# Sample-state updates that multiply 32 rows of keys and values in place of 128 masked ones, and pools that change hands in fewer steps

## The chip, the cores and the metric

The kernel runs on one core of a Trainium2 chip. The metric is the time of one execution on the device in microseconds, the median of several runs. TensorE is called PE, VectorE DVE, ScalarE ACT, GpSimd POOL and SyncE SP; SP and POOL issue the transfers between HBM and SBUF. PSUM, into which PE writes its sums, has eight banks of 512 float32 values in each of 128 partitions.

## The reference, cut to what matters

Two layers over 576 columns: 512 tokens of one prompt and 8 tokens of each of 8 sample rows. The first layer is a gated short convolution, the second a block with a matrix memory of 4 heads. The change touches the part in which the memory of each sample row is brought up to date (for a sample row, one chunk of 8 tokens):

```python
def step(carry, inp):                 # one chunk; for a sample row the only one
    C, n, m = carry
    ...
    logw = g[..., None] - b + ij
    m_new = jnp.maximum(g + m, jnp.max(logw, axis=-1))
    decay = jnp.exp(g + m - m_new)
    kw = kj * jnp.exp(logw - m_new[..., None])[..., None]
    C_new = decay[..., None, None] * C + jnp.einsum('bhjd,bhje->bhde', kw, vj)
    n_new = decay[..., None] * n + jnp.sum(kw, axis=2)
...
out = ((hn * onorm_w) + skip * xc) * jax.nn.silu(z)
return out @ w_out, new_buf, C, n, m
```

C has 8 rows x 4 heads x 512 x 512 values, 32 MB that are read, changed and written. `bhjd,bhje->bhde` sums over the 8 tokens of one sample row.

## The kernel before, in words

Values are float32. Products that have to be exact are split into a high and a low part (`hi`, `lo` of the activations, `wh`, `wl` of the weights) and made of three products. The large products of both layers (`p`, L311, 288 columns; `acc`, L229, 256 and 320 columns) run on PE one behind another; ACT makes `wh` (L209) and DVE `wl` (L210) from raw weight buffers that SP loads (L215). The kernel ends with a third stage, from about 1280 us on, in which the z gates (`acc`), the numerators and final states of the prompt (`num`, `cp`, L1214 and L1215) and the sample states lie side by side on every engine.

**Sample states.** `value_stack` and `key_stack` make for each head and each half u of the 8 sample rows a stack of 128 rows: 4 sample rows x 32, where the 32 are the 8 tokens in four forms (high and low parts of keys against high and low parts of values), so that one product over the 32 rows is the whole sum. `stack` (L1061 to L1063) scales the loaded keys (`ld`, fetched by SP at L1072), casts them to `sth` and subtracts, which gives `kst` or `vst`. `pn` (L1099) sums the keys. Then four copies `km` are made (L1107), each with all rows but those of one sample row set to zero by the constant `gmask`. There are 32 units (head, u, and one of 4 blocks dt of 128 keys) and 64 calls of `piece`, two to a unit, each for two sample rows j: the product `r` (L1160: weights are 128 columns of `km`, 512 columns of `vst` stream past them) and on DVE `c = c*dec + r` (L1161). A half state `c` is loaded at L172 and stored at L1130, both by SP.

**Tiles of the array.** PE can use a part of its rows or columns for a matmul. The trace writes the shape behind the names: 128*128 is the whole array; `qa` (L799) uses 32 of the columns (128*32) and puts four groups side by side; the corrections `Rs` (L1035, L1039) use 16 rows (16*128).

**Buffers.** One pool `act` of slots with the tag T holds `kst`, `vst`, `km`, `sth` and most others. `accumulators` closes a PSUM pool and opens the next, and whoever uses a bank of the new pool first waits for the last use of what lay there before. `load_buffers` does the same for the raw weight buffers and what lies beside them (scratch `X` of the first layer, then the states `C`). It is done at the start, within the first layer (`acc0a`), before its output projection (`acc0b`, `loads1`), at the second layer (`acc1`) and before the last stage (`acc2`, `loads2`). `mark` (L377) writes once to four block banks. The order of the rest is set by hand-written queues (`stream`, `work`, `pops`) and a scheduler that orders the instructions of each engine.

Of the kernel before, what the change touches and what calls it, by code (L numbers as in the profile page):

```python
# [40 lines left out]
CST = {}  # L41
_n = 0
for _name, _cnt in (("ident", 128), ("ones", 128), ("causal", 128), ("smask", 256), ("sel", 64),
                    ("seln", 4), ("gmask", 4), ("k_low", 1), ("v_low", 1), ("v_one", 2)):
    CST[_name] = (_n, _cnt)
    _n += _cnt
NCST = _n
# [2 lines left out]
HT = NT // 2  # L50
# [2 lines left out]
H0 = 4  # L53
H1 = 2
WARM2 = 14
CBUF = 8
LAG = 6
AHEAD = 2
FH = 2
# [9 lines left out]
def trunk(tc, io):  # L69
    nc = tc.nc  # L70
    ctx = ExitStack()
    with ctx:
# [2 lines left out]
        const = ctx.enter_context(tc.tile_pool(name="const", bufs=1))  # L75
        small = ctx.enter_context(tc.tile_pool(name="small", bufs=2))
        accs = [None, None]

        def accumulators(name, **kw):

            if accs[0] is not None:
                accs[0].close()
            accs[0] = ctx.enter_context(ExitStack())
            accs[1] = accs[0].enter_context(tc.tile_pool(name=name, space=PSUM, **kw))

        loads = [None, None, 0]

        def load_buffers(name, raw):

            if loads[0] is not None:  # L90
                loads[0].close()
            loads[0] = ctx.enter_context(ExitStack())
            loads[1] = loads[0].enter_context(tc.tile_pool(name=name, bufs=1))
            loads[2] = raw

        def load_tile(name, tag):
            uid[0] += 1
            return loads[1].tile([P, 2, 512], F32, name=f"{name}{uid[0]}", tag=tag, bufs=loads[2] if tag == "raw" else CBUF - loads[2])

        dram = ctx.enter_context(tc.tile_pool(name="dram", bufs=1, space=DRAM))  # L100

        uid = [0]
        layer0 = [False]

        def X(n=NT, name="x"):

            if not layer0[0]:
                return T(n, name=name)
            uid[0] += 1
            return loads[1].tile([P, n], F32, name=f"{name}{uid[0]}", tag="X", bufs=7)  # L110

        def T(n=NT, dt=F32, name="t"):
            uid[0] += 1
# [3 lines left out]
        def R(n=NT, name="r"):  # L117
            return T(n, F32R, name)

        def mm(name="mm"):  # L120
            uid[0] += 1
            return accs[1].tile([P, 1024], F32, name=f"{name}{uid[0]}", tag="mm", bufs=2)

        def block(name="blk"):
            uid[0] += 1
            return accs[1].tile([P, 512], F32, name=f"{name}{uid[0]}", tag="blk", bufs=4)[:, 0:HT]

        def bank(name="b"):
            uid[0] += 1
            return accs[1].tile([P, 512], F32, name=f"{name}{uid[0]}", tag="b1", bufs=4)  # L130

        def S(shape, dt=F32, name="s", bufs=2):
            uid[0] += 1
# [16 lines left out]
        def c(name, a=0, b=None):  # L150
            o, n = CST[name]
            return cst[:, o + a:o + (n if b is None else b)]
# [329 lines left out]
                ins = nc.tensor.matmul(b[:, 0:256], warm[:, 0:128], warm, start=True, stop=True).ins  # L482
            return ins

        accumulators("acc0", bufs=2)
        load_buffers("loads0", 4)
        layer0[0] = True
        warm_up(WARM)
        nc.scalar.preload_act_table_set("silu_and_others")
# [3 lines left out]
        for k in range(KD):  # L493
# [3 lines left out]
            if k in (0, 3):  # L497
                for c_ in range(2):
                    i = 4 * (k // 3)
# [53 lines left out]
        for f in range(NW):  # L553
            if f % 4 == 0:
                ext = T(320, name="ext")
                load(out=ext, in_=io["exa"][f // 4])
            ext_f = ext[:, 80 * (f % 4):80 * (f % 4) + 80].rearrange("p (b t) -> p b t", t=10)
            u, cv = T(name="u"), T(name="cv")

            def gated(u=u, c_=cx[0], x=cx[1]):  # L560
                nc.vector.tensor_tensor(c_, c_, rb2, ALU.mult)
                nc.vector.tensor_tensor(u, x, c_, ALU.mult)

            def saved(u=u, cv=cv, f=f):
                nc.gpsimd.tensor_copy(cpa[:, f, :], u[:, NP - 2:NP])
                nc.vector.tensor_tensor(cv, cv, rb, ALU.mult)

            work.append(gated)
            work.extend(conv_steps(cv, u, ext_f, [col("ca0", f), col("ca1", f), col("ca2", f)]))
            work.append(saved)  # L570

            second = f in SECOND
            if second:
                block_weights(4 * f + 2, 4 * f + 3)
            zb = [raw_weights(4 * f + i) for i in (2, 3)] if f and not second else None
            if f + 1 < NW:
                cx = [T(name="cx") if f < 11 else X(name="cx") for _ in range(2)]
            if f == 0:
                for i in range(2):
                    acc = mm("acc")  # L580
                    products(acc, weights(4 + i), h1, True, True)
                    nc.scalar.copy(cx[i], flat(acc))
                    if i:
                        block_weights(8, 9)
                    first_blocks(2 + i)
                accumulators("acc0a", bufs=2)
                mark(h1[0][0][:, 0:P], h1[0][0][:, 0:HT])
            elif f + 1 < NW:
                block_pair(4 * f + 4, 4 * f + 5, fs, None, *cx, False, pops=1)
            run(len(work))  # L590
            if 0 < f < NW - 2:
                block_weights(4 * f + 8, 4 * f + 9)

            def product(i):
                if f == 0:
                    return raws[i]
                acc = mm("acc")
                products(acc, weights(4 * f + i, raw=zb[i - 2]), h1, True, True)
                return flat(acc)

            z = T(name="z")
            if second:
                b_ = T(name="b")
                block_pair(4 * f + 2, 4 * f + 3, fs, None, z, b_, False)
                za = z
            else:
                za = product(2)
            nc.vector.tensor_tensor(z, za, rb, ALU.mult)
            nc.scalar.activation(z, z, AF.Silu)
            nc.vector.tensor_tensor(cv, b_ if second else product(3), cv, ALU.mult)  # L610
            nc.vector.tensor_tensor(cv, cv, z, ALU.mult)
            ya.append(split(cv))
            if f % 4 == 3:
                store(out=io["exa_out"][f // 4], in_=ext)
        accumulators("acc0b", bufs=2)
        load_buffers("loads1", 4)
        layer0[0] = False
        store(out=io["cpa_out"], in_=cpa)

# [26 lines left out]
        for f in range(NW):  # L646
# [84 lines left out]
        kss = [dram.tile([P, 2, 512], F32, name=f"kss{h}") for h in range(NH)]  # L731

        xc, fc = [], []
        accumulators("acc1", bufs=4)
        mark(xm[0][0][:, 0:P], xm[0][0][:, 0:HT])

        def later_tile(f):
# [7 lines left out]
        for h in range(NH):  # L745
            vt = []
            for dt in (0, 2):
                f = 4 * h + dt
# [101 lines left out]
        for h in (3, 0, 1, 2):  # L850
            st = heads[h]
            for dt in range(4):
                f = 4 * h + dt
# [40 lines left out]
            if h in (3, 0, 1):  # L894
                work.extend(lambda h=h, i=i: query_state(heads[h], unit(h, *divmod(i, 4)), i) for i in range(8))

        accumulators("acc2", bufs=2)
        load_buffers("loads2", 2)
        zs = {h: [] for h in range(NH)}

        def z_tile(pops=()):
# [151 lines left out]
        seln = const.tile([P, 4], F32R, name="seln")  # L1053
# [37 lines left out]
        def key_stack(h, u):  # L1091

            st = heads[h]
            raw, = fetched.pop(("ks", h, u))
            o = R(512, "kst")
            stack(raw, G["s"][:, 1 + u, 32 + 4 * h:33 + 4 * h], c("k_low"), o)
            pn = bank("pn")
            for dt in range(4):
                nc.tensor.matmul(pn[:, 4 * dt:4 * dt + 4], o[:, 128 * dt:128 * dt + 128], seln, start=True, stop=True)  # L1099
            t = S([P, 4, 4], name="ns")  # L1100
            nc.gpsimd.tensor_tensor(t, nst[:, h, u], G["dec"][:, 8 * h + 4 * u:8 * h + 4 * u + 4].unsqueeze(1)
                                    .broadcast_to([P, 4, 4]), ALU.mult)
            nc.vector.tensor_tensor(nst[:, h, u], pn[:, 0:16].rearrange("p (d g) -> p d g", g=4), t, ALU.add)

            st[u] = [R(512, "km") for _ in range(4)]
            for g, t in enumerate(st[u]):
                nc.scalar.activation(t, o.bitcast(F32), AF.Copy, scale=c("gmask", g, g + 1))  # L1107


        ORDER = (2, 0, 1, 3)  # L1110
# [24 lines left out]
        def piece(n):  # L1135
# [21 lines left out]
            o = 8 * h + 4 * u + 2 * i  # L1157
            for j in range(2):
                r = bank("r")
                nc.tensor.matmul(r, kst[2 * i + j][:, 128 * dt:128 * dt + 128], vst[:, 0:512], start=True, stop=True)  # L1160
                ins = nc.vector.scalar_tensor_tensor(ct[:, j, :], ct[:, j, :], dec[:, o + j:o + j + 1], r,  # L1161
                                                     ALU.mult, ALU.add).ins
                if j == 0:
                    store_half(ins)
# [338 lines left out]
def _consts():  # L1503
# [3 lines left out]
    def put(name, a):  # L1507
        o, n = CST[name]
        cst[:, o:o + n] = a
# [14 lines left out]
    sel[:, 32:48] = p[:, None] % 32 == 4 + r[None, :]  # L1524
    put("sel", sel)
    put("seln", ((g[:, None] == np.arange(4)[None, :]) & (s[:, None] % 2 == 0)).astype(np.float32))
    put("gmask", (g[:, None] == np.arange(4)[None, :]).astype(np.float32))
    ka, va = (s < 2).astype(np.float32), (s % 2 == 0).astype(np.float32)
    put("k_low", (ka - 1)[:, None])
    put("v_low", (va - 1)[:, None])  # L1530
# [106 lines left out]
```

## Time and profile before

| | |
|---|---|
| median of 3 runs | 1700.97 us (1699.05 to 1701.9) |
| profiled execution, own time | 1701.48 us |
| its span in the trace | 1699.6 us |
| PE busy | 1666.6 us (98%) |
| DVE busy | 1074.5 us (63%) |
| ACT busy | 749.6 us (44%) |
| POOL busy | 98.6 us (6%) |
| mean granted clock of PE | 0.989 |

The span runs from the first to the last instruction of the trace; the time of the execution holds 1.9 us more around it. A busy row of PE counts overlapping matmuls once. Starts of neighbouring rows tell what a matmul adds, since the shown duration of one overlaps the next.

### The profile page before, as it was taken

What the parts mean: (1) busy time and instruction counts of PE and PEld (TensorE: products, weight loads), DVE (VectorE), ACT (ScalarE), POOL (GpSimd) and SP (SyncE); (2) the same over time, 40 slices, a digit from 0 to 9 for tenths busy, and PEclk for the clock granted to TensorE, in tenths of its full rate; (3) what the DMA queues carried; (4) which work ended last, traced back from release to release, by engine and by line L of the source; (5) the groups of instructions that cost most, each with busy time, mean ns of one, the idle gap of its engine ahead of it and who ended that gap; (6) DMA issues with size and microseconds to landing.
All of it is one profiled execution on the core that took longest, in us unless ns stands there. A gap on an engine that the chain in (4) does not pass through costs nothing.

```text
span 1699.6 us, 30928 instructions
## 1 busy us (share of the span) xinstructions
PE 1666.6 (98%) x12251; PEld 1583.9 (93%) x12251; DVE 1074.5 (63%) x1957; ACT 749.6 (44%) x1463; POOL 98.6 (6%) x241
## 2 busy tenths in 40 slices
PE   9999999999999999999999999999999999997998
PEld 8999999999999999999999899899898788897998
DVE  7988888874337975556644345344367567776775
ACT  5555555542234554444533233233245456554431
POOL 0000000000000000000010000000002100000000
PEclk9999999999999999999999999999999899998999
DMA  5222322314333444535433652642746587998993
GB/s 195 75 91 92 104 86 97 103 53 163 128 116 94 141 128 123 172 112 173 131 88 98 220 162 75 234 139 66 252 143 208 197 286 262 321 331 265 324 326 105
DMA packets 107488, 275.23 MB, mean 162 GB/s; under 512 B 11056, under 2 KB 33456, under 8 KB 107344
## 3 DMA queue, kind: packets, MB, share of 16 engines
q1 hardware_dynamic: 91984, 255.95, 45.8%
q10 hardware_dynamic: 15360, 17.32, 2.9%
q8 instruction: 96, 1.57, 0.4%
q14 instruction: 48, 0.39, 0.1%
HBM read 211.13 MB, written 62.09 MB: 161 GB/s over the span
## 4 chain that ended last, share of the span: by engine, by line
PE 91%; DMA 4%; DVE 2%; ACT 1%; issue 1%; SPq 0%; DVEq 0%; ACTq 0%
PE acc L229 31%; PE p L311 29%; PE p L387 17%; PE qa L799 2%; DMA c<-cs 2%; PE r L1160 1%; PE g L700 1%; PE cp L1214 1%; PE ta L719 1%; DMA cs_out<-c 1%; PE cp L1215 1%; PE blk L387 1%; PE s L818 1%; DMA wr<-wts 1%; PE s L819 0%
## 5 line engine op out<-in xcount | busy, mean ns | idle before, releaser
L311 PE MATMUL p<-hi,wh 128*128 128x288 f32 x1136 | 337.3, 297 | 0.0
L311 PE MATMUL p<-lo,wh 128*128 128x288 f32 x1136 | 334.0, 294 | 0.0
L311 PE MATMUL p<-hi,wl 128*128 128x288 f32 x1136 | 333.6, 295 | 0.0
L209 ACT CAST wh<-wr 128x512 fp32r<-128x512 f32 x262 | 161.8, 620 | 324.0 <-PE acc L229 170.7
L229 PE MATMUL acc<-hi,wh 128*128 128x256 f32 (+1 forms) x1328 | 290.2, 299 | 6.8 <-ACT num L1227 3.9
L210 DVE TENSOR_TENSOR wl<-wr,wh 128x512 fp32r<-128x512 f32 x262 | 179.5, 688 | 176.5 <-ACT wh L209 171.9
L229 PE MATMUL acc<-lo,wh 128*128 128x256 f32 (+1 forms) x1328 | 289.0, 298 | 0.0
L229 PE MATMUL acc<-hi,wl 128*128 128x256 f32 (+1 forms) x1328 | 288.3, 298 | 0.0
L229 PEld LDWEIGHTS acc<-hi,wh 128*128 128x128 f32 x1328 | 225.0, 191 | 12.4 <-ACT num L1227 4.1
L229 PEld LDWEIGHTS acc<-hi,wl 128*128 128x128 f32 x1328 | 224.3, 191 | 2.0 <-issue 1.7
L229 PEld LDWEIGHTS acc<-lo,wh 128*128 128x128 f32 x1328 | 224.8, 191 | 0.8 <-issue 0.6
L311 PEld LDWEIGHTS p<-hi,wh 128*128 128x128 f32 x1136 | 213.1, 188 | 6.3 <-ACT wh L209 5.0
L311 PEld LDWEIGHTS p<-hi,wl 128*128 128x128 f32 x1136 | 212.5, 188 | 3.8 <-issue 2.5
L311 PEld LDWEIGHTS p<-lo,wh 128*128 128x128 f32 x1136 | 213.3, 188 | 0.0
L257 ACT CAST wh<-wr 128x512 fp32r<-128x512 f32 x176 | 109.0, 619 | 200.5 <-PE p L311 99.6
L257 ACT CAST wh<-ws 128x512 fp32r<-128x512 f32 x132 | 81.9, 620 | 197.2 <-PE p L387 98.1
L258 DVE TENSOR_TENSOR wl<-wr,wh 128x512 fp32r<-128x512 f32 x176 | 121.3, 689 | 67.4 <-ACT wh L257 58.4
L387 PE MATMUL p<-hi,wl 128*128 128x288 f32 x736 | 160.1, 297 | 0.0
L387 PE MATMUL p<-hi,wh 128*128 128x288 f32 x736 | 159.7, 298 | 0.0
L387 PE MATMUL p<-lo,wh 128*128 128x288 f32 x736 | 159.7, 296 | 0.0
L258 DVE TENSOR_TENSOR wl<-ws,wh 128x512 fp32r<-128x512 f32 x132 | 91.0, 689 | 105.1 <-ACT wh L257 91.9
L387 PEld LDWEIGHTS p<-hi,wh 128*128 128x128 f32 x736 | 117.9, 188 | 9.7 <-issue 8.0
(382 smaller groups left out, 2582.2 us busy)
## 6 DMA issues: line engine op xcount, KB each, us to landing
wr<-wts SPq DMA_DIRECT2D x222, 512.0 KB, 3.7
c<-cs SPq DMA_DIRECT2D x112, 512.0 KB, 5.6
cs_out<-c SPq DMA_DIRECT2D x64, 512.0 KB, 6.7
x<-xT SPq DMA_DIRECT2D x16, 288.0 KB, 4.4
xcs<-xc ACTq DMA_DIRECT2D x16, 288.0 KB, 2.3
x<-xcs SPq DMA_DIRECT2D x16, 288.0 KB, 4.3
ld<-xcs SPq DMA_DIRECT2D x16, 288.0 KB, 8.0
cp_out<-cp ACTq DMA_DIRECT2D x16, 257.0 KB, 7.3
```

What stands on the lines that cost most here:

```text
L209: last_act[0] = nc.scalar.copy(hi, raw[:, 4 * i:4 * i + 4, :]).ins
L210: nc.vector.tensor_tensor(lo, raw[:, 4 * i:4 * i + 4, :], hi.bitcast(F32), ALU.subtract)
L229: nc.tensor.matmul(acc[:, o:o + j - i], a[:, k % 4, :], x[:, i:j], start=(first and k == 0 and p == 0), stop=(last and k == 7 and p == 2))
L257: last_act[0] = nc.scalar.copy(hi, src).ins
L258: nc.vector.tensor_tensor(lo, src, hi.bitcast(F32), ALU.subtract)
L311: nc.tensor.matmul(bank_, a[:, j, :], x, start=(start and j == 0 and i == 0), stop=(j == 3 and i == 2), skip_group_check=True)
L387: nc.tensor.matmul(b, a[:, k % 4, :], x[:, t:t + HT], start=bool(new) and k == 0 and i == 0, stop=(k == 7 and i == 2), skip_group_check=True)
L700: nc.tensor.matmul(g[32 * j:32 * j + 32, 0:b - a], w[:, 32 * j:32 * j + 32], tiles[j][:, a:b], start=True, stop=True)
L719: nc.tensor.transpose(pa[:, 128 * it:128 * it + 128], t[:, 128 * it:128 * it + 128], ident)
L799: nc.tensor.matmul(st["q"][32 * g:32 * g + 32, :], st["qp"][dt // 2][:, dt % 2, 128 * u + 32 * g:128 * u + 32 * g + 32], ct[g // 2][:, g % ...
L818: nc.tensor.matmul(sb[0], a[:, 0:128], b[:, 0:512], **ends)
L1160: nc.tensor.matmul(r, kst[2 * i + j][:, 128 * dt:128 * dt + 128], vst[:, 0:512], start=True, stop=True)
```

## The change

- The product `r` takes the 32 rows of its sample row, `kst[g]` and `vst[g]` with `g` 32 rows wide at 0, 32, 64 or 96, so the four sample rows use four row tiles of the array. The 32 copies `km`, their slots and `gmask` are gone.
- PSUM: block banks and the others have a pool each. The pool `acc0a` goes on through the output projection of the first layer, so `acc0b` is gone; there `bank()` takes block banks (`bank_tag`). `acc1` replaces the two wide accumulators alone, and the block banks that `mark` writes stay as they are.
- SBUF: the raw weight buffers `raw0` stay open over the first layer and its output projection; only the scratch X makes room for the states C (`scratch0`, `states1`). Before the last stage both are replaced (`raw2`, `states2`), as before.

```diff
+        bank_tag = ["b1"]
+        def accumulators(name, blocks=None):
+            for i in (1,) if blocks is None else (1, 0):
+                if accs[i] is not None:
+                    accs[i][0].close()
+                    accs[i] = None
+            for i in (0, 1) if blocks else (1,):
+                stack = ctx.enter_context(ExitStack())
+                accs[i] = stack, stack.enter_context(tc.tile_pool(name=f"{name}{i}", bufs=4, space=PSUM))
+        def load_buffers(tag, name, bufs=None):
+            for t in ("C", "raw") if tag == "raw" else ("C",):
+                if t in loads:
+                    loads.pop(t)[0].close()
+            stack = ctx.enter_context(ExitStack())
+            loads[tag] = stack, stack.enter_context(tc.tile_pool(name=name, bufs=1)), bufs
...
-            return accs[1].tile([P, 512], F32, name=f"{name}{uid[0]}", tag="b1", bufs=4)
+            return accs[bank_tag[0] == "b1"][1].tile([P, 512], F32, name=f"{name}{uid[0]}", tag=bank_tag[0], bufs=4)
...
-                accumulators("acc0a", bufs=2)
+                accumulators("acc0a", True)
+                bank_tag[0] = "blk"
...
-        accumulators("acc0b", bufs=2)
-        load_buffers("loads1", 4)
+        load_buffers("C", "states1", 4)
...
-        accumulators("acc1", bufs=4)
+        accumulators("acc1")
+        bank_tag[0] = "b1"
         mark(xm[0][0][:, 0:P], xm[0][0][:, 0:HT])
...
-            st[u] = [R(512, "km") for _ in range(4)]
-            for g, t in enumerate(st[u]):
-                nc.scalar.activation(t, o.bitcast(F32), AF.Copy, scale=c("gmask", g, g + 1))
+            st[u] = o
...
-                nc.tensor.matmul(r, kst[2 * i + j][:, 128 * dt:128 * dt + 128], vst[:, 0:512], start=True, stop=True)
+                g = slice(32 * (2 * i + j), 32 * (2 * i + j) + 32)
+                nc.tensor.matmul(r, kst[g, 128 * dt:128 * dt + 128], vst[g, 0:512], start=True, stop=True)
```

Lines of the new kernel stand 1 to 6 further down (`r` L1164, `acc` L232, `pn` L1105, key loads L1078, loads and stores of states L175 and L1133).

The scheduler also moves instructions. On PE, up to the first `r` of the program, the order is the same in both. After it the `r`s and the work among them are mixed anew. This is PE where the keys of a later head come in, in the kernel before (names carry a running number):

```order
10372 L1215 MATMUL cp_17459<-vl_16800,hi_17375 128x256
10373 L1099 MATMUL pn_17421<-seln,kst_17416 128x4 x4
10374 L1160 MATMUL r_17439<-vst_15197,km_16887 128x512
10375 L1160 MATMUL r_17443<-vst_15197,km_16888 128x512
10376 L1160 MATMUL r_17486<-vst_15197,km_16889 128x512
10377 L1160 MATMUL r_17490<-vst_15197,km_16890 128x512
10378 L1160 MATMUL r_17557<-vst_16292,km_17429 128x512
10379 L1160 MATMUL r_17561<-vst_16292,km_17430 128x512
10380 L1160 MATMUL r_17619<-vst_16292,km_17431 128x512
10381 L229 MATMUL acc_17508<-hi_14647,wh_17511 128x256
```

and in the changed one:

```order
10371 L1219 MATMUL cp_17426<-vl_16783,hi_17350 128x256
10372 L232 MATMUL acc_17475<-hi_14649,wh_17478 128x256
10373 L232 MATMUL acc_17475<-hi_14649,wh_17478 128x320
...
10389 L232 MATMUL acc_17475<-hi_14659,wl_17479 128x320
10390 L232 MATMUL acc_17475<-hi_14664,wh_17478 128x256
10391 L1105 MATMUL pn_17396<-seln,kst_17391 128x4 x4
10392 L1164 MATMUL r_17406<-vst_15204,kst_16857 128x512
10393 L1164 MATMUL r_17410<-vst_15204,kst_16857 128x512
10394 L1164 MATMUL r_17453<-vst_15204,kst_16857 128x512
10395 L232 MATMUL acc_17475<-hi_14664,wh_17478 128x320
```

Nineteen products of the z gates now stand ahead of `pn`, and three `r`s in a row behind it where there were seven.

On SP, the place is the load of the last head's keys (`ld<-kss`) among loads and stores of half states (`c<-cs`, `cs_out<-c`), in the kernel before:

```order
528 L1130 DMA cs_out<-c_17819 128x1024
529 L1130 DMA cs_out<-c_17920 128x1024
530 L172 DMA c_18195<-cs 128x1024
531 L1130 DMA cs_out<-c_18005 128x1024
532 L1072 DMA ld_18107<-kss_7132 128x512
533 L172 DMA c_18231<-cs 128x1024
```

and in the changed one:

```order
528 L1133 DMA cs_out<-c_17786 128x1024
529 L1133 DMA cs_out<-c_17887 128x1024
530 L1078 DMA ld_18066<-kss_7134 128x512
531 L175 DMA c_18154<-cs 128x1024
532 L1133 DMA cs_out<-c_17964 128x1024
533 L175 DMA c_18190<-cs 128x1024
```

The key load now comes directly behind the two stores, ahead of a load and a store that it followed.

Counted over the whole order of PE, it goes from one shape of tile to another 173 times before and 315 times in the changed kernel; from the first `r` on it is 63 and 205. The 128 `r`s stand there in 81 runs without anything between: 45 of one, 27 of two, 7 of three and 2 of four, and no two neighbours within a run use the same 32 rows.

## Rows read from the trace of the kernel before

**Rows 1.** The page: span, and section 1, busy time of each engine.

```profile
span 1699.6 us, 30928 instructions
...
PE 1666.6 (98%) x12251; PEld 1583.9 (93%) x12251; DVE 1074.5 (63%) x1957; ACT 749.6 (44%) x1463; POOL 98.6 (6%) x241
```

**Rows 2.** Windows: busy us of PE, PEld, DVE, ACT, POOL; granted clock; DMA; GB/s.

```profile
1325.00:1338.70 13.70, 13.70 (x80) 8.82 (x76) 6.29 (x9) 4.28 (x8) 0.00 (x0) 1.00 0.39 136
...
1338.70:1349.00 10.30, 10.30 (x38) 7.24 (x37) 7.83 (x14) 5.31 (x13) 0.19 (x1) 0.50 0.55 189
...
1499.10:1502.50 3.40, 3.37 (x12) 2.83 (x13) 3.40 (x6) 1.83 (x4) 0.00 (x0) 0.51 0.78 202
...
1500.00:1536.00 36.00, 36.00 (x260) 35.60 (x260) 25.43 (x50) 17.59 (x37) 1.35 (x2) 0.96 0.99 352
...
1567.40:1574.20 6.80, 6.08 (x24) 5.88 (x25) 4.01 (x12) 3.50 (x11) 0.37 (x2) 0.50 0.97 303
...
1595.00:1660.00 65.00, 65.00 (x475) 63.76 (x473) 45.60 (x73) 21.70 (x40) 0.00 (x0) 1.00 0.95 335
```

**Rows 3.** Grouped lines: update products, masked keys: count | busy, mean ns | idle before.

```profile
L1160 PE MATMUL r<-vst,km 128*128 128x512 f32 x128 | 49.4, 448 | 3.8 <-DVE c L1161 2.6 <-DVE nst L1103 0.6 <-ACT y L1287 0.5
...
L1107 ACT ACTIVATE km<-kst,cst 128x512 fp32r<-128x512 f32 x32 | 20.6, 712 | 6.8 <-DVE kst L1063 6.8
```

**Rows 4.** Timeline of PE, steady r's (start, duration of the row, operation, [idle before]).

```profile
1649.93 0.63 PE L1160 MATMUL r<-vst,km 128*128 128x512 f32 x2
...
1650.40 0.42 PE L229 MATMUL acc<-hi,wh 128*128 128x320 f32 x2
```

**Rows 5.** Timeline of PE around column tiles of 32 (128*32).

```profile
1333.01 0.43 PE L229 MATMUL acc<-lo,wh 128*128 128x256 f32 x2
...
1333.28 0.42 PE L229 MATMUL acc<-hi,wl 128*128 128x256 f32 x2
...
1333.63 1.06 PE L799 MATMUL qa<-c,qp 128*32 128x512 f32 x8
...
1334.63 0.50 PE L1160 MATMUL r<-vst,km 128*128 128x512 f32 x1
...
1334.97 0.22 PE L1033 MATMUL d<-masks 128*128 128x128 f32 x1
```

**Rows 6.** Timeline of PE, row tiles of 16 keys (16*128), then r.

```profile
1331.09 0.45 PE L1039 MATMUL d<-Rs,masks 16*128 16x256 f32 x2
...
1331.46 0.50 PE L1160 MATMUL r<-vst,km 128*128 128x512 f32 x1
```

**Rows 7.** Timeline at the two hand-overs of banks: PE, DVE, PE.

```profile
389.99 0.50 PE L229 MATMUL acc<-hi,wh 128*128 128x256 f32 x2 [0.94 <-DVE cv L610]
...
599.88 0.69 DVE L258 TENSOR_TENSOR wl<-wr,wh 128x512 fp32r<-128x512 f32 x1
...
600.24 0.79 PE L377 MATMUL mark<-hi 128*128 128x288 f32 x4 [0.98 <-ACT xm L660]
```

**Rows 8.** Timeline of ACT and PE, 1490 to 1501.

```profile
1494.99 0.62 ACT L1062 CAST sth<-ld 128x512 fp32r<-128x512 f32 x1 [3.01 <-DMA cp_out<-cp]
...
1496.45 0.61 PE L1099 MATMUL pn<-seln,kst 128*128 128x4 f32 x4 [1.08 <-DVE kst L1063]
...
1496.92 1.19 PE L1160 MATMUL r<-vst,km 128*128 128x512 f32 x4
...
1500.22 0.68 PE L229 MATMUL acc<-hi,wh 128*128 128x256 f32 x2
```

**Rows 9.** Timeline of SP's queue, ACT and PE, 1550 to 1570.

```profile
1553.08 2.33 SPq L1130 DMA_DIRECT2D cs_out<-c  x2
...
1560.98 0.42 SPq L1072 DMA_DIRECT2D ld<-kss  x1
...
1566.88 0.72 ACT L1061 ACTIVATE ld<-ld,cols 128x512 f32<-128x512 f32 x1 [8.11 <-DMA ld<-kss]
...
1568.12 0.85 PE L229 MATMUL acc<-hi,wh 128*128 128x256 f32 x2 [3.94 <-ACT num L1227]
```

More of the change, by code (lines that the diff above doesn't have):

```diff
@@ L43 @@
 for _name, _cnt in (("ident", 128), ("ones", 128), ("causal", 128), ("smask", 256), ("sel", 64),
-                    ("seln", 4), ("gmask", 4), ("k_low", 1), ("v_low", 1), ("v_one", 2)):
+                    ("seln", 4), ("k_low", 1), ("v_low", 1), ("v_one", 2)):
     CST[_name] = (_n, _cnt)
@@ L55 @@
 WARM2 = 14
-CBUF = 8
 LAG = 6
@@ L77, in trunk @@
         accs = [None, None]
[L79 to L94, printed above, removed]
+        bank_tag = ["b1"]
[7 more added lines that the diff above has]
+                accs[i] = stack, stack.enter_context(tc.tile_pool(name=f"{name}{i}", bufs=4, space=PSUM))
+        loads = {}
+        def load_buffers(tag, name, bufs=None):
[4 more added lines that the diff above has]
+            loads[tag] = stack, stack.enter_context(tc.tile_pool(name=name, bufs=1)), bufs
         def load_tile(name, tag):
             uid[0] += 1
-            return loads[1].tile([P, 2, 512], F32, name=f"{name}{uid[0]}", tag=tag, bufs=loads[2] if tag == "raw" else CBUF - loads[2])
+            return loads[tag][1].tile([P, 2, 512], F32, name=f"{name}{uid[0]}", tag=tag, bufs=loads[tag][2])
         dram = ctx.enter_context(tc.tile_pool(name="dram", bufs=1, space=DRAM))
@@ L109, in X @@
             uid[0] += 1
-            return loads[1].tile([P, n], F32, name=f"{name}{uid[0]}", tag="X", bufs=7)
+            return loads["C"][1].tile([P, n], F32, name=f"{name}{uid[0]}", tag="X", bufs=7)
         def T(n=NT, dt=F32, name="t"):
@@ L121, in mm @@
             uid[0] += 1
-            return accs[1].tile([P, 1024], F32, name=f"{name}{uid[0]}", tag="mm", bufs=2)
+            return accs[1][1].tile([P, 1024], F32, name=f"{name}{uid[0]}", tag="mm", bufs=2)
         def block(name="blk"):
             uid[0] += 1
-            return accs[1].tile([P, 512], F32, name=f"{name}{uid[0]}", tag="blk", bufs=4)[:, 0:HT]
+            return accs[0][1].tile([P, 512], F32, name=f"{name}{uid[0]}", tag="blk", bufs=4)[:, 0:HT]
         def bank(name="b"):
             uid[0] += 1
-            return accs[1].tile([P, 512], F32, name=f"{name}{uid[0]}", tag="b1", bufs=4)
+            return accs[bank_tag[0] == "b1"][1].tile([P, 512], F32, name=f"{name}{uid[0]}", tag=bank_tag[0], bufs=4)
         def S(shape, dt=F32, name="s", bufs=2):
@@ L483, in warm_up @@
             return ins
-        accumulators("acc0", bufs=2)
-        load_buffers("loads0", 4)
+        accumulators("acc0", False)
+        load_buffers("raw", "raw0", 4)
+        load_buffers("C", "scratch0")
         layer0[0] = True
@@ L895, in trunk @@
                 work.extend(lambda h=h, i=i: query_state(heads[h], unit(h, *divmod(i, 4)), i) for i in range(8))
-        accumulators("acc2", bufs=2)
-        load_buffers("loads2", 2)
+        accumulators("acc2", False)
+        load_buffers("raw", "raw2", 2)
+        load_buffers("C", "states2", 6)
         zs = {h: [] for h in range(NH)}
@@ L1526, in _consts @@
     put("seln", ((g[:, None] == np.arange(4)[None, :]) & (s[:, None] % 2 == 0)).astype(np.float32))
-    put("gmask", (g[:, None] == np.arange(4)[None, :]).astype(np.float32))
     ka, va = (s < 2).astype(np.float32), (s % 2 == 0).astype(np.float32)
```

## The prediction

> **What bounds the kernel now.** Read the page first: PE is busy for 1666.6 us of a span of 1699.6 [rows 1], so nothing else can be long on the path, and what counts is how long PE takes for each thing and where it waits. Before the third stage the change leaves PE's order as it is, so there it can only take away waits. In the third stage it changes the 128 matmuls `r` and what stands round them; they are 49.4 us of PE's busy row, with only 3.8 us of idle time ahead of them [rows 3]. Then the windows [rows 2]: in the 65 us from 1595 PE is busy for all 65, and the transfers have 0.95 of their engines at work; from 1500 to 1536 it is 36 of 36 and 0.99. So in these stretches PE's own work sets the time, with the transfers hardly behind it. The column of the granted clock has a second thing to see: at 1.00 in one stretch it is 0.50, which is 1.2 in place of 2.4 GHz, from 1338.7 to 1349.0, in 1499.1 to 1502.5 and in 1567.4 to 1574.2.
>
> The execution took 1701.48 us for a span of 1699.6; the median of the runs is 1700.97, so 0.5 us less than what the sum below starts from. About 0.2% (3.4 us) is what a measurement of this kernel can tell from no change.
>
> **The hand-overs: -1.4.** At 389.99 the first `acc` of the output projection waits 0.94 for `cv`, the last reader of a bank in the pool that closes [rows 7]. Without that closing it waits only for the gate that was read earlier: -0.9. At 600.24 `mark` waits 0.98 for ACT's `xm` [rows 7]. In the changed kernel its banks are free, but the products behind it need the low weights `wl`, which DVE makes from 599.88 for 0.69 us, so to 600.57 [rows 7]. `mark` takes 0.63 us (to the next start), so it can begin where PE stood at about 599.3 and fill the wait, and the products start at about 600.6 in place of 600.87: -0.3 to -0.6, I take 0.5. Both lie on the path, since PE does nothing else then. The raw buffers that stay open let four weight loads be issued earlier; no row shows PE waiting for them there, so nothing.
>
> **The masked keys: 0.** 32 copies of 0.71 us, 20.6 us in all, go from ACT [rows 3]. ACT is busy for 44% of the span, and PE's idle time ahead of `r` names DVE, not ACT, for most of it, so the cover is ACT's own slack; where ACT is late they count in the waits below.
>
> **The tiles: +8.7.** An `r` of 512 columns steadily adds 0.235 us (two of them from 1649.93 to 1650.40 [rows 4]). With 32 rows it streams the same 512 columns, so a single one gets no shorter. Two things change. First, the shape of the tile. The trace of before has no `r` with 32 rows, but it has other small tiles, and shows what they cost around them. Two `acc` take 0.27 (1333.01 to 1333.28), but 0.35 where `qa` with 32 columns follows (1333.28 to 1333.63): going in costs 0.08 to 0.09. The `r` that follows `qa` takes 0.34 in place of 0.235 (1334.63 to 1334.97 [rows 5]): 0.10 behind the return. The two `Rs` of 16 rows and 256 columns take 0.37 (1331.09 to 1331.46 [rows 6]) against 0.27 for the two `acc`: 0.08 to 0.10 on leaving. Together some 0.27 us for in and out. The order has 142 more changes of shape, 71 times in and out: 71 x 0.27 = 19.2. Some fall where PE waits anyhow (about 10, by the waits named below and the others between 1410 and 1430 and 1536 and 1575): 61 x 0.27 = 16.5.
>
> Second, neighbours in a run use different rows, 47 such pairs. Eight `qa`s of 512 columns in four column groups take 1.00 us (1333.63 to 1334.63 [rows 5]), of which 0.08 for leaving: 0.46 for each set of four, against 4 x 0.235 = 0.94 one behind another. So the tiles run side by side; each after the first adds between nothing (if the rest of the 0.46 is the change from the first set's weights to the second's) and (0.46 - 0.235)/3 = 0.075. For rows in place of columns no row shows it, and the bounds are wider: from nothing to 0.235 (no overlap at all). I take 0.04, in the middle of the nearest rows: a pair saves 0.195. Of 47 some 7 stand where PE waits anyhow: 40 x 0.195 = -7.8. Together +8.7; without overlap +16.5.
>
> The Trainium skill's page "TensorEngine Tiling (Array Packing)", in Tiling Modes, Key Properties, says that a change of tiling mode drains the engine while different tiles may load and multiply in parallel. By this the change pays a drain at each edge of a run and gains only within a run, as the rows 5 and 6 have it. "TensorE: Matmul & The Clock Gate" gives 3.07 times for four row tiles of 512 columns; as an estimate from it, four `r`s would take 0.94 / 3.07 = 0.31, so each further one 0.02, and the sum would be +7.9 in place of +8.7.
>
> **Two waits in the third stage: -6.7.** At 1494.99 ACT casts the next keys (`sth`) only when a transfer of `cp` has landed, 3.01 us late, since it needs that slot; `pn` then waits 1.08 us on PE at 1496.45, and the seven `r`s behind it take from 1496.92 to 1500.22, 3.30 us where 7 x 0.235 = 1.64 would do, as DVE takes up each [rows 8]. With the slots of `km` free the cast waits only for earlier work of DVE; and products of the z gates stand ahead of `pn`, with three `r`s behind it. So 1.08 + 1.66 = 2.7 can go. At 1566.88 ACT gets the keys of the last head 5.9 us after SP issued their load at 1560.98; behind them ACT's `num` is late, and PE waits 3.94 us at 1568.12 [rows 9]. SP's two stores ahead of it in the new order end at about 1555.4 [rows 9], so the load is issued up to 5.6 us earlier and the wait of 3.94 goes. Late next there is DVE or the next `acc`'s weights. All this is PE's idle time on the path.
>
> **The clock: -2.4.** Behind both waits the clock falls to 0.50: 3.4 us from 1499.1 and 6.8 from 1567.4 [rows 2]. If it stays up, half of each is won, 1.7 and 3.4. Part of the second stretch is idle (6.08 of 6.8 busy), so 3.0. Together up to 4.7; the stretch from 1338.7 shows that it can fall with no idle time ahead, so I take half.
>
> **Sum:** -1.4 + 8.7 - 6.7 - 2.4 = -1.8. From 1701.48 that is 1699.7, and by the median 1699.2: 0.1% less, which can't be told from no change. Chance 0.33, with its own range of 1696 to 1703 (the clock all or not at all, the pairs at 0 to 0.075).
>
> **Rivals.**
> - *Faster: pairs cost nothing further and the relief reaches other waits* (0.25). Pairs at 0: 40 x 0.235 = 9.4, so tiles +7.1; the clock given back in full, -4.7; half of the 3.8 us that `r` waited [rows 3], 2 us: -1.4 + 7.1 - 6.7 - 4.7 - 2 = -7.7, so 1693.3 by the median. For it: ACT loses 20.6 us in the very stage where it is waited for. Against: the transfers at 0.95 to 0.99.
> - *Slower: row tiles don't run side by side* (0.17). All of them add their columns to one set of sums, unlike the column tiles of rows 5. Each further `r` at 0.235: tiles +16.5, sum +6.0, so 1707.0; at 0.11, the middle, +1.0 and no change. It decides from about 0.17 a pair (-1.8 + 40 x 0.13 = 3.4).
> - *No change: the transfers take the gain back* (0.17). With 0.99 busy from 1500 to 1536 and 0.95 from 1595 [rows 2], a PE that comes sooner waits for states. Then the 2.7 at 1496 and the clock come back as a wait, and about 59 of the 205 edges in these stretches are hidden, some 2.5 us: -1.4 + 6.2 - 3.9 = +0.9, so 1701.9.
> - *Slower: the clock falls more often* (0.08). From 1325 to 1338.7 PE is busy for 13.70 of 13.70 at 1.00, with many small tiles, and then it is at 0.50 for 10.3 us [rows 2]; no row shows idle time as its cause. If small tiles are the cause, twice 5 us more at half clock cost 5: 1704.2. Against: the tiles of rows 5 at 1.00.
>
> The rule on drains alone, with all waits as before, would be the change that only costs: -1.4 + 8.7 = +7.3, so 1708; it needs both waits to stay, which the order speaks against, and counts with the second rival.
>
> **From these:** faster by over 0.2% (under 1697.6): the first rival and a third of the likeliest's, 0.36. Slower (over 1704.4): the second, the fourth and 0.01 of the rest, 0.26. Within 0.2%: 0.38. The range from 1691 to 1709 leaves out the far end of the first rival and several things going wrong together.
>
> **What would show it.** PE starts at 390 and 600 with 0.9 and about 0.5 us less wait; a pair of `r`s in a run starts 0.01 to 0.08 us apart where the tiles run together, 0.235 where they don't; the `acc` behind an `r` adds some 0.1 more than its steady price, as does the one ahead; SP issues the last head's keys some 5 us earlier against `num`; PE's idle times of 1.08 and 3.94 are gone; the clock is 1.00 behind them. Wrong it would be if the edges cost far from 0.27, if pairs don't overlap, or if states (`c`) become what DVE and then PE wait for.

## The result, and the profile after

The changed kernel takes 1705.94 us (median of 8 runs, 1703.87 to 1709.32), the kernel before 1699.43 beside it (1695.35 to 1704.76): ratio 1.0040, with an interval from 1.0023 to 1.0057. It is slower by about 0.4%. Forecast were 1699.2 and no measurable change.

The page after, span and PE's busy time, to be held against [rows 1]:

```profile
span 1704.5 us, 30872 instructions
PE 1681.9 (99%) x12251; PEld 1582.3 (93%) x12251; DVE 1075.1 (63%) x1957; ACT 731.5 (43%) x1431; POOL 100.4 (6%) x241
```

PE is busier by 15.3 us and the span longer by 4.9, so PE waits less and works longer. The third stage is taken to begin with the last four `ta`, the transposes of the last keys, at 1279.2 before and at 1278.0 after. The windows from there to the end (length, then busy time of PE, PEld, DVE, ACT and POOL, granted clock, share of the transfers, GB/s), first before, then after, each with stretches of it by themselves:

```profile
1279.20:1699.60 420.40, 396.04 (x2743) 360.98 (x2743) 291.62 (x589) 198.02 (x420) 20.55 (x42) 0.96 0.76 261
1372.90:1376.30 3.40, 3.40 (x17) 3.40 (x17) 2.02 (x6) 1.57 (x6) 0.00 (x0) 0.51 1.01 322
1550.30:1557.10 6.80, 4.70 (x16) 3.65 (x16) 6.80 (x12) 0.00 (x0) 0.00 (x0) 0.50 0.83 241
```

```profile
1278.00:1704.50 426.50, 411.30 (x2743) 359.12 (x2743) 293.09 (x589) 179.23 (x388) 21.73 (x42) 0.95 0.75 257
1336.40:1353.40 17.00, 16.72 (x61) 11.92 (x61) 9.88 (x17) 5.62 (x13) 0.38 (x2) 0.50 0.57 195
1373.90:1380.70 6.80, 6.80 (x29) 6.14 (x30) 2.54 (x6) 2.36 (x8) 0.00 (x0) 0.50 0.85 262
1431.90:1438.80 6.90, 6.58 (x25) 5.42 (x24) 5.76 (x15) 0.28 (x1) 0.00 (x0) 0.51 0.94 360
1499.10:1502.50 3.40, 3.40 (x31) 3.40 (x30) 2.18 (x5) 1.92 (x4) 0.00 (x0) 1.00 1.03 361
1524.10:1527.50 3.40, 3.40 (x17) 3.40 (x16) 2.98 (x5) 0.33 (x1) 0.18 (x1) 0.50 1.04 410
1550.30:1557.10 6.80, 6.80 (x45) 5.74 (x44) 6.80 (x13) 3.52 (x7) 0.00 (x0) 1.00 0.51 175
1565.10:1568.50 3.40, 3.40 (x15) 2.74 (x13) 3.33 (x8) 0.00 (x0) 0.00 (x0) 0.50 0.72 266
```

The stage starts 1.2 us sooner and lasts 6.1 longer. PE's idle time in it falls from 24.4 (420.40 - 396.04) to 15.2, so 9.2 less, and its busy time rises by 15.3. Half of PE's busy time at a clock of 0.50, summed over the whole trace, is 15.6 us before and 20.1 after, so 4.5 of the 15.3 are the clock, and 10.8 are work.

That work is the edges of the runs. The timeline of PE, a run of two and a run of one (start, duration of the row):

```profile
1466.26 0.28 PE L232 MATMUL acc<-hi,wl 128*128 128x256 f32 x1
1466.47 0.49 PE L1164 MATMUL r<-vst,kst 32*128 32x512 f32 x1
1466.89 0.41 PE L232 MATMUL acc<-hi,wl 128*128 128x320 f32 x1
...
1654.08 0.43 PE L232 MATMUL acc<-hi,wl 128*128 128x320 f32 x2
1654.44 0.50 PE L1164 MATMUL r<-vst,kst 32*128 32x512 f32 x2
1654.87 0.54 PE L232 MATMUL acc<-hi,wh 128*128 128x320 f32 x2
1655.24 0.43 PE L232 MATMUL acc<-lo,wh 128*128 128x320 f32 x2
```

Two `r`s take 0.43 us to the next start, and so does one (1466.47 to 1466.89): the second is free. But the two `acc` ahead take 0.36 in place of 0.27, those behind 0.37. So every run costs 0.62 us: 0.09 on the way in, 0.43, and 0.10 behind. The kernel before paid 0.23 for one `r` and 0.47 for two [rows 4], where nothing held them up.

At these prices 81 runs would cost 81 x 0.62 - 128 x 0.234 = 20.3 us more than before, and PE's work grew by 10.8. One reason is in the kernel before: from the start of a run of `r`s to the next other matmul it took 47.8 us in all, and not 128 x 0.234 = 30.0, since many of its `r`s waited for DVE, in part under rows that the busy time counts as work. After the change the same sum is 46.4. How the rest is shared out between waits and edges was not followed run by run.

Against [rows 7], the hand-overs:

```profile
389.71 0.43 PE L232 MATMUL acc<-hi,wh 128*128 128x256 f32 x2
...
597.95 0.69 PE L380 MATMUL mark<-hi 128*128 128x288 f32 x4
598.48 0.43 PE L314 MATMUL p<-hl,wh 128*128 128x288 f32 x2
```

Neither wait is there, and the products of the second layer start at 598.48 where they stood at 600.87. Of these 2.4 us half is lost again in the second layer, where `qa` waits 1.4 us in three places for states (0.4 in one before), here as PE's list of waits has them, after, then before (total, times, longest):

```profile
PE qa L804 <- DMA c<-cs: 1.4, 3, 0.6
```

```profile
PE qa L799 <- DMA c<-cs: 0.4, 1, 0.4
```

Against [rows 9], SP, ACT and PE around the last head's keys:

```profile
1563.47 0.42 SPq L1078 DMA_DIRECT2D ld<-kss  x1
...
1563.08 1.07 ACT L1231 COPY num<-num 128x514 f32<-128x514 f32 x2
1568.80 0.72 ACT L1067 ACTIVATE ld<-ld,cols 128x512 f32<-128x512 f32 x1 [4.65 <-DMA ld<-kss]
...
1572.01 0.43 PE L232 MATMUL acc<-hi,wh 128*128 128x256 f32 x2
```

PE's wait of 3.94 is gone, though the keys are loaded later than before (1563.47 against 1560.98): on ACT two `num` now stand ahead of the `ld` that waits for the keys. (Both traces show the transfers issued by SP and ACT, and none by POOL.)

### The profile page after: what moved, and what is told of

Its sections match the earlier page's. It is cut to its first block, busy times and chain, and to the rows that moved or that the text cites. A ratio compares the mean times of both kernels' runs of the same rounds, so it can differ in the third digit from the quotient of the medians.

```text
span 1704.5 us, 30872 instructions
## 1 busy us (share of the span) xinstructions
PE 1681.9 (99%) x12251; PEld 1582.3 (93%) x12251; DVE 1075.1 (63%) x1957; ACT 731.5 (43%) x1431; POOL 100.4 (6%) x241
## 4 chain that ended last, share of the span: by engine, by line
PE 92%; DMA 4%; DVE 2%; ACT 1%; issue 1%; SPq 0%; DVEq 0%; ACTq 0%
PE acc L232 31%; PE p L314 29%; PE p L390 17%; PE qa L804 2%; DMA c<-cs 2%; PE r L1164 2%; PE cp L1218 1%; PE cp L1219 1%; PE g L704 1%; DMA wr<-wts 1%; PE ta L723 1%; PE blk L390 1%; PE s L823 1%; DVE c L1165 1%; PE num L1218 1%
## 5 line engine op out<-in xcount | busy, mean ns | idle before, releaser
L232 PE MATMUL acc<-hi,wh 128*128 128x256 f32 (+1 forms) x1328 | 292.5, 301 | 1.8 <-DVE xm L662 1.6
L232 PE MATMUL acc<-lo,wh 128*128 128x256 f32 (+1 forms) x1328 | 289.3, 298 | 0.0
L232 PE MATMUL acc<-hi,wl 128*128 128x256 f32 (+1 forms) x1328 | 288.8, 298 | 0.0
L232 PEld LDWEIGHTS acc<-hi,wh 128*128 128x128 f32 x1328 | 222.3, 190 | 12.3 <-issue 10.2
L232 PEld LDWEIGHTS acc<-hi,wl 128*128 128x128 f32 x1328 | 223.9, 190 | 3.1 <-issue 2.7
L232 PEld LDWEIGHTS acc<-lo,wh 128*128 128x128 f32 x1328 | 223.9, 190 | 1.9 <-issue 1.9
```

The source lines that it names most:

```text
L232: nc.tensor.matmul(acc[:, o:o + j - i], a[:, k % 4, :], x[:, i:j], start=(first and k == 0 and p == 0), stop=(last and k == 7 and p == 2))
```

## The experiments

All are compared with the kernel before, run on the same chip. "Lost to the clock" is, for one execution, one less its mean granted clock, times its time; the mean over the executions stands with its standard error. One number needs it first: the kernel before loses 19.0 ± 0.8 (the 17 executions beside runs 5 to 8) and takes 1682.4 without that loss; the changed kernel loses 23.2 ± 0.6 (8) and takes 1682.9 without it. By this count nearly the whole net difference is the clock, 4.2 of 4.7 us. The 8 executions of the kernel before that ran beside the changed one have no clock on record; their mean is 1699.3, 6.8 us under that of the changed kernel. If they too took 1682.4 without the loss, which no record shows, they lost 16.9, and the clock made 6.3 of the 6.8.

**1. The 32-row products alone** (no masked copies, old pools).

```diff
 # the kernel before, with
-            st[u] = [R(512, "km") for _ in range(4)]
...
+            st[u] = o
+                g = slice(32 * (2 * i + j), 32 * (2 * i + j) + 32)
+                nc.tensor.matmul(r, kst[g, 128 * dt:128 * dt + 128], vst[g, 0:512], start=True, stop=True)
```

> The kernel before with the 32-row products alone (no masked copies), pools and weight buffers as they were. Theory 1 (the tiles cost the time: a run of r's of any length takes 0.62 us with its edges, where one r took 0.23 and two 0.46; the hand-overs save 1.2 to 1.9): slower than the kernel before by 6 to 10 us, ratio 1.0035 to 1.006, and the two waits of 0.94 and 0.98 at the hand-overs are there again. Theory 2 (the new pools and the order that they bring cost the time): ratio 0.997 to 1.001.

Measured: 1710.29, ratio 1.0053 (1.0032 to 1.0074), lost to the clock 23.1 ± 2.3 (1687.2 without it). Both hand-over waits are there:

```profile
389.97 0.50 PE L229 MATMUL acc<-hi,wh 128*128 128x256 f32 x2 [0.94 <-DVE cv L610]
...
600.22 0.79 PE L377 MATMUL mark<-hi 128*128 128x288 f32 x4 [0.98 <-ACT xm L660]
```

So it is the tiles that cost.

**2. The new pools alone** (masked copies and 128-row products).

```diff
 # the changed kernel, with
-            st[u] = o
+            st[u] = [R(512, "km") for _ in range(4)]
+            for g, t in enumerate(st[u]):
+                nc.scalar.activation(t, o.bitcast(F32), AF.Copy, scale=c("gmask", g, g + 1))
```

> The changed kernel with the 32 masked copies and 128-row products put back, so the pools and weight buffers are the only change. Theory 1: the hand-overs save 1.2 to 1.9 us, ratio 0.9985 to 0.9995, no difference that can be measured. Theory 2: slower by 4 us or more, ratio over 1.002.

Measured: 1692.91, ratio 0.9956 (0.9940 to 0.9972), lost to the clock 14.1 ± 0.8. Better than either theory said: faster than both kernels, though the copies are still made. With run 1 it shows that the two gains don't add: pools and tiles each take idle time out of the third stage, which is 24.4 before, 15.4 in run 1, 20.5 in run 2 and 15.2 with both.

**3. The same kernel without change of tile.**

```diff
 # the changed kernel, with
-                g = slice(32 * (2 * i + j), 32 * (2 * i + j) + 32)
-                nc.tensor.matmul(r, kst[g, 128 * dt:128 * dt + 128], vst[g, 0:512], start=True, stop=True)
+                nc.tensor.matmul(r, kst[:, 128 * dt:128 * dt + 128], vst[:, 0:512], start=True, stop=True)
```

> The changed kernel with its order, but each r multiplies all 128 rows of the stacks, without masks: this leaves out the separation of the four sample rows (the products add all four), so only its time is read. No change of tile, no copies. Theory 1 with the clock tied to the small tiles: some 10.7 us of edges and the 4.5 us of lower clock go, 1690 to 1695, ratio 0.994 to 0.997, and less time at half clock than the 45.9 us of the changed kernel (38.7 before). Theory 1 with the clock tied to something else (waits, chance): ratio 0.995 to 0.999 and half clock still 40 to 50 us. Rival (DVE and the transfers set the pace of the third stage, so PE's time comes back as waits): ratio 1.000 to 1.004, PE idle time up by 8 us or more.

Measured: 1688.13, ratio 0.9923 (0.9906 to 0.9939), lost to the clock 14.4 ± 0.7. Its third stage:

```profile
1277.50:1686.50 409.00, 391.34 (x2743) 359.70 (x2743) 292.02 (x589) 178.89 (x388) 21.04 (x42) 0.96 0.77 269
```

With 81 runs of `r`s as in the changed kernel (the order among the other work differs in places), PE is busy 20.0 us less, and idle for 17.7, only 2.5 more. Of the 20.0, 6.4 are the clock (half of the busy time at 0.50 is 13.7) and 13.6 work. The edges and the clock are real costs, and little comes back as a wait.

Runs 2 and 3 differ in their source by the masked copies alone (the scheduler's order follows). On one chip they are 4.8 us apart, or 6.0 without the clock loss (1679.7 and 1673.7), and their intervals don't overlap.

**4. Four in a run.** The four `r`s of a unit are issued together, each after DVE has added the unit before.

```diff
 # the changed kernel, with, in piece(n) of the second half of a unit
+            rs = [bank("r") for _ in range(4)]
+            for k in range(4):
+                g = slice(32 * k, 32 * k + 32)
+                mi = nc.tensor.matmul(rs[k], kst[g, 128 * dt:128 * dt + 128], vst[g, 0:512], start=True, stop=True).ins
+                if sums_of:
+                    tc.add_manual_dep(mi, sums_of[-1].name, mybir.DependencyInfo(
+                        mybir.DependencyClass.Sync, mybir.DependencyReason.DATA))
+            for k in range(4):
...
+            sums_of.append(ins)
```

> The changed kernel with the four r's of a unit issued together, each waiting until the unit before has been added by DVE, so that they stand in 54 runs in place of 81 (17 of four, 9 of three, 5 of two, 23 of one). Theory 1: 27 runs less at 0.62 us each is 16.7 us less of PE's time; with a few us given back as waits for DVE 1690 to 1698, ratio 0.994 to 0.999 to the kernel before. Rival (a run's time grows with its length by 0.1 us or more for each r, or the wait for DVE takes the place): 1702 to 1708, ratio 1.002 to 1.005.

Measured: 1708.95, ratio 1.0045 (1.0027 to 1.0063). The timeline of PE:

```profile
1646.72 0.43 PE L232 MATMUL acc<-hi,wl 128*128 128x320 f32 x2
1647.08 0.51 PE L1168 MATMUL r<-vst,kst 32*128 32x512 f32 x4
1647.52 0.54 PE L232 MATMUL acc<-hi,wh 128*128 128x320 f32 x2
```

and its third stage and PE's longest waits:

```profile
1277.30:1705.20 427.90, 403.97 (x2743) 355.89 (x2743) 290.76 (x589) 179.28 (x388) 24.97 (x42) 0.94 0.75 257
```

```profile
PE r L1168 <- DVE c L1173: 4.7, 5, 1.6
PE hb L1299 <- DVE c L1173: 2.7, 1, 2.7
PE r L1168 <- DVE nst L1109: 2.6, 1, 2.6
```

The price of a run was right: four take 0.44 as one does. The time was not: PE is busy only 7.3 us less than in the changed kernel where 16.7 were forecast, idle time goes from 15.2 to 23.9, and 27.3 ± 1.1 us are lost to the clock. Most of the new idle time is waits for DVE: the last two lines are new, and the first was 4.2 in the changed kernel.

**5. Copies on GpSimd**, pools as in run 2.

```diff
-                nc.scalar.activation(t, o.bitcast(F32), AF.Copy, scale=c("gmask", g, g + 1))
+                nc.gpsimd.tensor_scalar(t, o.bitcast(F32), c("gmask", g, g + 1), None, ALU.mult)
```

> The new pools with 128-row products from masked copies, the copies made by GpSimd in place of ScalarE. Theory (ScalarE's late work in the third stage costs PE some 3 to 5 us, as between the runs with copies and with 128 unmasked rows): 1686 to 1692, ratio 0.991 to 0.995, PE idle time in the third stage 10 to 12 us against 14.0 with the copies on ScalarE. Rival (GpSimd's copies come later than ScalarE's, and PE waits for them, or they slow DVE down): 1695 to 1705, ratio 0.997 to 1.002, with idle time ahead of r put down to POOL.

Measured: 1690.98, ratio 0.9941 (0.9925 to 0.9957). In the forecast range, but not for its reason: idle time in the third stage is 21.8 (20.5 in run 2; the 14.0 of the expectation leaves out the 6.5 us behind the last matmul), and the two ratios' intervals overlap. A copy takes 1.79 us on GpSimd, where ScalarE needs 0.71 [rows 3]. So this run doesn't show that ScalarE's copies were a cost. Runs 2 and 3 speak for one, with the order changed as well.

**6. 64 rows, and 7. rows 0 to 31 for all.**

```diff
 # 6
+                g = slice(64 * j, 64 * j + 64)
 # 7
+                g = slice(0, 32)
```

> The changed kernel with 64 rows of the stacks to each product in place of 32 (rows 0 to 63 for the first sample row of a piece, 64 to 127 for the second); each product then adds two sample rows, so the separation of the sample rows is left out and only the time is read. If the price lies in the change of tile shape alone: a run costs 0.62 us as with 32 rows, the time at half clock is 45 us or more, 1703 to 1709. If the price or the clock goes by the rows that lie idle: a run costs clearly less, or the time at half clock falls to 32 to 40 us, 1690 to 1701.

> The changed kernel, its order on every engine the same, with rows 0 to 31 for every product: the sums of three of the four sample rows are left out. No two r's of a run use different rows. If the runs of the changed kernel are cheap because different rows work side by side: a second r in a run adds 0.1 to 0.3 us here (against 0.004), 47 such pairs make 5 to 13 us, 1710 to 1719, ratio 1.006 to 1.012. If a second r is cheap for another reason (already paid by the drain): 0.00 to 0.05 us and 1703 to 1709.

Measured: run 6 1701.02, ratio 0.9997 (0.9985 to 1.0010), lost to the clock 15.2 ± 0.4; run 7 1713.28, ratio 1.0073 (1.0046 to 1.0100), lost 23.7 ± 3.5. The timelines of PE, run 6, then run 7:

```profile
1644.87 0.50 PE L1164 MATMUL r<-vst,kst 64*128 64x512 f32 x2
1645.31 0.53 PE L232 MATMUL acc<-hi,wh 128*128 128x320 f32 x2
```

```profile
1650.43 0.73 PE L1164 MATMUL r<-vst,kst 32*128 32x512 f32 x2
1651.08 0.53 PE L232 MATMUL acc<-hi,wh 128*128 128x320 f32 x2
```

Two `r`s in the same rows take 0.65 to the next start, in different rows 0.43 or 0.44, and three in the same rows take 0.89:

```profile
1601.39 0.96 PE L1164 MATMUL r<-vst,kst 32*128 32x512 f32 x3
1602.28 0.39 PE L1218 MATMUL cp<-vh,hi 128*128 128x256 f32 x1
```

So runs are cheap because different rows work side by side, and an edge costs the same with 64 rows as with 32: its price lies in the change of shape. Run 6 has these edges and is as fast as the kernel before; its loss to the clock is 8 us less than that of the changed kernel (in another set of runs), which speaks against the edges alone as the cause of that loss.

**8. The new PSUM pools alone.**

> The kernel before with the new PSUM pools alone; copies, 128-row products and weight buffers are as before. The run with both kinds of pools was 0.9956 of the kernel before, which the two hand-overs (1.2 us net by the start of the third stage) explain only in part; the rest is a shorter third stage in a new order. If PSUM's pools bring that order: ratio 0.994 to 0.998. If the weight buffers do: 0.998 to 1.001, with the hand-over waits at 390 and 600 gone but the third stage as long as before (413.6 us).

```diff
 # run 2, with
-        load_buffers("raw", "raw0", 4)
-        load_buffers("C", "scratch0")
+        load_buffers("loads0", 4)
...
-        load_buffers("C", "states1", 4)
+        load_buffers("loads1", 4)
...
-        load_buffers("raw", "raw2", 2)
-        load_buffers("C", "states2", 6)
+        load_buffers("loads2", 2)
```

Measured: 1692.72, ratio 0.9947 (0.9930 to 0.9964), lost to the clock 13.3 ± 0.5. So the PSUM pools bring all that run 2 has. Its third stage lasts 412.7 us in place of 420.4 (the 413.6 of the expectation counts, within 0.3 us, to the end of the last matmul):

```profile
1277.30:1690.00 412.70, 391.71 (x2743) 356.80 (x2743) 291.37 (x589) 198.30 (x420) 20.77 (x42) 0.97 0.77 266
```

Idle time is 21.0 (24.4 before), with the copies still made.

**9 to 12. The clock, by rows.** Run 4 with 64 rows (9) and 128 rows (10) to each product, and runs 4 and 9 once more beside each other on one chip (11, 12). The orders of 4 and 9 are the same on PE, DVE, ACT and SP.

```diff
 # run 4, with
-                g = slice(32 * k, 32 * k + 32)
+                g = slice(64 * (k % 2), 64 * (k % 2) + 64)      # 9
+                g = slice(0, 128)                               # 10
```

> The run with the four r's of a unit together, the order on every engine the same, with 64 rows in place of 32 to each product (two sample rows added in each, so their separation is left out). Two of the four use rows 0 to 63 and two 64 to 127, so a run of four takes longer, some 0.1 to 0.35 us each, 17 runs: 2 to 6 us more work of PE. Theory (the clock goes by how many rows the products use): less time lost to the clock than the 27.3 us of the 32-row run (mean over its runs), 15 to 20 us, so 1698 to 1707. Rival (the waits for DVE lower the clock, whatever the rows): 25 to 30 us lost, 1709 to 1715.

> The same grouping of four, each waiting for the unit before, with all 128 rows to each product and no masks (the separation of the sample rows left out); no change of tile. The four now take 0.93 us one behind another. Theory (rows): 13 to 17 us lost to the clock, 1693 to 1700. Rival (waits): 23 us or more, 1702 to 1710.

> The four r's of a unit together with 32 rows each, once more, beside the 64-row version on the same chip, since the two were run on different chips. If the rows lower the clock: 25 to 30 us lost to the clock on average here and 15 to 21 for 64 rows, times within 2 us of each other or this one slower. If it was the chip: both lose the same within 3 us, and this one is the faster by the 8 us less work of PE.

> The 64-row version with the same order, beside the 32-row one on the same chip (the sums of two sample rows fall together, so their separation is left out). If the rows lower the clock: 15 to 21 us lost to it. If it was the chip: the same loss as the 32-row version within 3 us, and slower by some 8 us.

| run | rows | median, us | ratio (interval) | lost to the clock, us | time without it |
|---|---|---|---|---|---|
| 9 | 64 | 1705.98 | 1.0026 (1.0010 to 1.0042) | 18.8 ± 1.5 | 1687.3 |
| 10 | 128 | 1697.20 | 0.9969 (0.9955 to 0.9983) | 17.1 ± 0.4 | 1679.6 |
| 11 | 32 | 1704.87 | 1.0016 (0.9998 to 1.0034) | 22.0 ± 1.4 | 1682.5 |
| 12 | 64 | 1707.54 | 1.0033 (1.0016 to 1.0051) | 19.3 ± 1.4 | 1687.0 |

A run of four with 64 rows takes 0.67 us, since two and two follow each other:

```profile
1649.38 0.74 PE L1168 MATMUL r<-vst,kst 64*128 64x512 f32 x4
1650.05 0.53 PE L232 MATMUL acc<-hi,wh 128*128 128x320 f32 x2
```

Runs 9 and 10 came out as the theory of rows said. Runs 11 and 12, the cleanest pair, don't decide it: 2.7 us between them, with an error of 2.0. Run 11 lost less than the 25 to 30 that its expectation had for this theory. It is run 4 once more, and loses 22.0 where run 4 lost 27.3 on another chip, 5.3 us apart with an error of 1.8. So a difference of some 5 us between kernels on different chips proves little by itself.

## Why the prediction was wrong

**The clock** is the step that failed: "Behind both waits the clock falls to 0.50 ... If it stays up, half of each is won ... so I take half", -2.4. The waits went, and the clock loss rose by 4.2 us (19.0 to 23.2 over the executions; 4.5 in the two profiles). That missed 6.6 to 6.9 us. The forecast itself was off by 6.7 in the time and by 8.3 in the change (-1.8 against +6.5), and no other term missed by more than 2.5. Behind the two waits it came true in part: in the profile 1499.1 is at 1.00 after the change, around 1567 there are 3.4 us at half clock in place of 6.8, and 6.8 us from 1550.3 are gone as well. But the stretch from 1338.7, with PE busy all the time ahead of it [rows 2], went from 10.3 us to 17.0 (now from 1336.4), the one from 1372.9 from 3.4 to 6.8, and new ones stand at 1431.9, among `r`s, and at 1524.1. I tied the half clock to idle time. The row from 1338.7 showed it with none, and I took that only as a reason to halve the gain, not as a loss that could grow. The rival "the clock falls more often" had named this, with 1704.2, and got 0.08.

How far this goes with the small tiles: on one chip, runs 2 and 3 with 128 rows lose 14.1 and 14.4, and runs 1 and 4 with 32 rows 23.1 and 27.3. In all that have the new pools it is 13.3 to 17.1 with 128 rows (runs 2, 3, 5, 8, 10), 15.2 to 19.3 with 64 (6, 9, 12) and 22.0 to 27.3 with 32 (after, 4, 7, 11). That the kernels with 32-row products lose more than those with whole-array ones and the new pools is shown: the two ranges lie apart. What in them does it is not: orders and waits differ too, and no pair of 32 and 128 rows on one chip has the same order. That 32 rows lose more than 64 is likely by the ranges, but the pair on one chip leaves it open. Rows are not all of it: the kernel before loses 19.0 with 128 rows, in another order, 4.1 less than run 1 on the same chip with an error of 2.5.

**The other terms** summed to +0.6 and measured +0.5 (1682.4 to 1682.9 without the clock loss), but not one by one:
- Tiles, +8.7 forecast, 10.8 measured. "Together some 0.27 us for in and out" was too low: 0.62 for a run of one against 0.23 is 0.39. The way in (0.09) and behind (0.10) were right; leaving is 0.19 and not 0.08. I had read it from two `Rs` of 256 columns and 16 rows, where an `r` has 512 and 32; which of the two makes the difference was not tried. A pair saves the whole 0.23, not 0.195. With these prices the prediction's own counts give 61 x 0.39 - 40 x 0.234 = 14.4, which misses the 10.8 by more than the forecast did. So the sum came near partly by luck: edges priced too low, and `r`s of the kernel before taken at 0.234 each, where waits for DVE made them dearer. The second rival (no overlap) is refuted by 0.43 for one and for two; run 7 shows what it would have cost.
- Waits, -6.7 forecast; the whole idle time of the stage fell by 9.2. The waits of 1.08 and 3.94 are gone. The reason given for the second, "the load is issued up to 5.6 us earlier", was wrong: it is issued 2.5 us later, and ACT's order hides it. So that part of the term came true by luck.
- Hand-overs, -1.4 forecast, -1.2 at the start of the third stage: more was won at 600 (2.4 with the first), half given back to waits for states.
- Masked keys, 0 forecast: open. Run 3 is 4.8 us faster than run 2, which makes the copies; run 5, with the copies on GpSimd, lies between them. What the changed kernel won by it is contained in the waits above.

A run of one costs 0.39 us more than on the whole array, and one, two and four take 0.43 to 0.44. The Trainium skill, "TensorEngine Tiling (Array Packing)", Tiling Modes, Key Properties, says that a change of mode drains the engine and that different tiles run in parallel. The trace agrees: each run pays 0.39 us at its edges, and a second `r` in other rows adds nothing, where in the same rows it adds 0.22. The Trainium skill, "TensorE: Matmul & The Clock Gate", Measured speedup vs the span model, gives 3.07 times for four row tiles; here four `r`s gain 0.94 / 0.44 = 2.1 times, with the way out counted in.

The third rival, transfers that take the gain back, finds no support: run 3 is 0.8% faster with the same states to move.

What stays open is why the PSUM pools shorten the third stage (run 8). Its order, its idle time (3.4 us less) and its clock (5.7 us less lost) differ; which of them brings which was not tried.

## What to carry to other kernels

A product with few rows costs no less than one with all; it pays only where enough of them stand side by side. Here a run cost 0.62 us at any length to four and a whole-array product 0.23, so three in a run gain little (0.62 against 0.70), and 72 of 81 runs were shorter. Masked copies on an engine with slack were the cheaper way here, if not free: the new pools with the copies took 0.9947 to 0.9956 of the time before. Price the clock by what other kernels in the record show at the same shapes, not by where idle time stands.

## What the runs showed of the hardware that was not expected

- Executions of one kernel can differ mainly by their clock: run 12 took 1699.5 at a mean granted clock of 0.992 and 1712.0 at 0.985, and its 12 times spread over 12.5 us with the clock loss and over 3.9 without. In run 10 it was not so (6.1 and 6.6). Without the loss, the kernel before takes 1682.3 to 1683.0 in the mean on each of four chips.
- Leaving a small tile cost 0.19 us behind an `r` of 32 rows and 512 columns, more than the 0.08 to 0.10 read behind `Rs` of 16 rows and 256 columns.
- Products in the same 32 rows take 0.43, 0.65 and 0.89 us to the next start for one, two and three, against 0.23, 0.47 and 0.70 on the whole array: each further one costs as much there as on the whole array, and the 0.19 more is paid once a run.
